# Feed-forward gate and up as 2x2 block products: seven products of 256 columns for eight

## The chip, the cores and the metric

The kernel runs on one core of one Trainium2 chip. It is a two-layer model step in one launch. Time is device time in microseconds (us) of that core; lower is better. TensorE does the matrix products (the profile lists matmuls as PE, weight loads as PEld), VectorE is DVE, ScalarE is ACT, GpSimd is POOL, and SyncE (SP) issues most transfers. Each engine works through its own queue in order and waits on semaphores for the others.

## The reference

```python
# x: 512 tokens, D_MODEL = 1024, D_FF = 2816, all float32
def swiglu(x, w_gate, w_up, w_down):
    return (jax.nn.silu(x @ w_gate) * (x @ w_up)) @ w_down
...
x = x + concat([o_nsa, o_mla], axis=-1) @ ev_w_out[i]          # layer 0: attention mixers
x = x + swiglu(rms_norm(x, ev_ffn_norm[i]), ffn_w_gate[i], ffn_w_up[i], ffn_w_down[i])
...
x = x + short_conv_mixer(u, b_g, c_g, conv_w[i]) @ od_w_out[i]  # layer 1
x = x + moe_swiglu(rms_norm(x, od_ffn_norm[i]), ...)
```

The change is in the `swiglu` of layer 0 alone.

## The kernel before

The stages follow each other: attention mixers, their output projection (`out_rest`), the feed-forward part, the convolution layer, the experts. Every fp32 matrix product is made of three: each operand is split into a rounded part `hi` and a remainder `lo`, and `mm3` issues hi·hi, hi·lo and lo·hi into one PSUM sum. A split is one ACT cast (`hi`) and one DVE subtraction (`lo`).

**Weights.** `Weights` holds one list of pieces for the whole kernel in the order of use. A piece arrives by an SP transfer of 512 KB (128x1024) in one of six raw buffers (`wbr0` to `wbr5`), is split into one of six part buffers (`wap0` to `wap2`, `wbp0` to `wbp2`), and then its raw buffer takes the next transfer. `done(...)` gives part buffers back and calls `pump`, which writes down the next transfers and splits in each engine's queue at that place of the program. So the order of `done` calls sets where a split stands between other work.

**Feed-forward part.** `FFN_ORDER` lists 22 "up" tiles (128 of the 2816 columns of gate and of up, all 512 tokens) and six "down" products: up 0, 1, 2, 3, down of tiles 0 and 1, then runs of four up tiles with a down of four tiles behind each, and at last up 20, 21 and a down of 18 to 21. Tiles 0 and 1 go through `first`, in products of 256 tokens, with the transposes of the last two token blocks between them. Tiles 2 to 21 take `product_of_next` for gate and again for up (8 blocks of depth 128, three matmuls of 512 columns each, so 48 matmuls a tile), and `ff_tile`:

```python
ACT.activation(sg, pg, AF.Silu)
DVE.tensor_tensor(sg, pu, sg, op=OP.mult)
split(hT[f][:, 0], hT[f][:, 1], sg)
```

**Ahead of it.** `out_rest` interleaves the output projection with the norm of each of four token blocks: squares on ACT, a sum on DVE, a power on POOL (`rs`, in `norm.factor`), the scaling to `xn` on DVE (`norm.scale`), PE transposes of `xn` into PSUM (`pt`), and the split of those into the activations `b0h`, `b0l`, `b1h`, `b1l`. Transposes 0 and 1 are in `out_rest`, 2 and 3 in `first`. POOL has nothing but the four powers there.

Of the kernel before, what the change touches and what calls it, by code (L numbers as in the profile page):

```python
# [302 lines left out]
class Weights:  # L303
# [22 lines left out]
    def add_part(self, src, offset, row, at, k, n, keep=False):  # L326

        self.pieces.append(Piece(len(self.chunks), 0, k, n, keep))
        self.chunks.append((bass.AP(tensor=src.tensor, offset=src.offset + offset + at, ap=[[row, 128], [1, k * n]]), k * n))

    def pump(self, pieces=99):

        while True:
            if self.loaded < len(self.chunks) and self.raw_free:
                ap, m = self.chunks[self.loaded]
                pool, tag = slot = self.raw_free.pop(0)
                t = pool.tile([128, PW], F32, name=tag, tag=tag, bufs=1)
# [3 lines left out]
            elif (pieces and self.ready < len(self.pieces) and self.pieces[self.ready].chunk in self.raw  # L341
                  and self.part_free):
                pieces -= 1
                p = self.pieces[self.ready]
                self.ready += 1
                raw, raw_slot = self.raw[p.chunk]
                pool, tag = p.slot = self.part_free.pop(0)
                p.t = pool.tile([128, 2, PW], F32R, name=tag, tag=tag, bufs=1)
                m = p.k * p.n
                src = raw[:, p.at:p.at + m]  # L350
                self.nc.scalar.copy(p.t[:, 0, :m], src)  # L351
                self.nc.vector.tensor_tensor(p.t[:, 1, :m], src, p.t[:, 0, :m].bitcast(F32), op=OP.subtract)  # L352
                if p.keep:
                    p.raw, p.raw_slot = self.raw.pop(p.chunk)
                else:
                    self.raw_free.append(self.raw.pop(p.chunk)[1])
            else:
                return

    def use(self):  # L360

        while self.ready <= self.used:
            before = self.ready
            self.pump(1)
            assert self.ready > before
        self.used += 1
        return self.pieces[self.used - 1]

    def done(self, *pieces, splits=99):
        self.part_free += [p.slot for p in pieces]  # L370
        self.pump(splits)

    def let_go(self, *pieces):
# [12 lines left out]
class Piece:  # L386
# [40 lines left out]
def kernel(ctx: ExitStack, tc: tile.TileContext, A, out, stop=None):  # L427
# [32 lines left out]
    def weight_room(name, raw, parts):  # L460
        W.room(wx.enter_context(tc.tile_pool(name=name, bufs=1, side="right")), raw, parts)
# [23 lines left out]
    og = od = 0  # L485
    for do, f in FFN_ORDER:
        if do == "up":
            og = W.add(A["w_gu"], og, (KD, 128), (KD, 128))
# [91 lines left out]
    with ExitStack() as l0:  # L580
# [686 lines left out]
        oT = Act.of([b() for b in oh], [b() for b in ol])  # L1267
        W.resume(len(chunk_bufs), 3)

    weight_room("wb", 6, 3)  # L1270
    rt = wx.enter_context(tc.tile_pool(name="rt", bufs=1, side="right"))
    psA = ctx.enter_context(tc.tile_pool(name="psA", bufs=4, space=PSUM))
# [136 lines left out]
        return p  # L1409

    def ff_tile(f, pg, pu):
        sg = work.tile([128, T], F32, name="sg", bufs=2)
        hT[f] = work.tile([128, 2, T], F32R, name="hT", tag="hT", bufs=6)
        ACT.activation(sg, pg, AF.Silu)
        DVE.tensor_tensor(sg, pu, sg, op=OP.mult)
        split(hT[f][:, 0], hT[f][:, 1], sg)

    def ff_down(f0, nf, mid, end):
# [47 lines left out]

    def conv_tile(j, pc, pu, pb):
        z = zs[j % 2]
        ct = work.tile([128, T], F32, name="sg", bufs=2)
# [63 lines left out]
    def transpose(i):  # L1533

        hl = split_rows[i] = [work.tile([128, KD, 128], F32R, name="hT", tag="hT", bufs=6) for _ in range(2)]
        for b in range(2):
            pt = psA.tile([128, 4, 128], F32, name="pt", tag="p")
            for j in range(4):
                k = 4 * b + j
                PE.transpose(pt[:, j], xr[i][:, k * 128:(k + 1) * 128], ident)  # L1540
            split(hl[0][:, 4 * b:4 * b + 4], hl[1][:, 4 * b:4 * b + 4], pt)

    def logits(i):
        h, l = split_rows.pop(i)
# [7 lines left out]
        lT = work.tile([16, 128], F32, name="sg", bufs=2)  # L1552
        ACT.copy(lT, p)
        return lT

# [477 lines left out]
```

## Time and profile before

| | |
|---|---|
| median of 3 runs | 1367.07 us (1365.72 to 1367.53) |
| the profiled execution's own time | 1367.42 us |
| its span | 1365.7 us |
| PE busy in the span | 1332.3 us (98%) |
| DVE, ACT, POOL busy | 844.6 us (62%), 688.8 us (50%), 208.2 us (15%) |
| stretch 358 to 691 us (up tiles 2 to 21 and downs): PE, DVE, ACT, POOL busy | 333.00, 131.53, 88.11, 1.65 of 333 us |
| granted TensorE clock, whole span | 0.994 of full speed |

The span is the part of the execution in which instructions ran; the 1.7 us beside it lie outside. A matmul's recorded duration overlaps the next one's, so the pace of PE is read from the distance of starts, not from the durations. A row of the timeline gives start, duration, engine, line, operation, output<-inputs with the shape, and in brackets how long the engine had been idle and for whom it waited.

### The profile page before, as it was taken

How to read it: one execution, taken by the hardware profiler on the slowest of the kernel's cores; microseconds unless marked ns; L12 is line 12 of the kernel's file. 1: busy time of each engine (PE TensorE's matmuls, PEld its weight loads, DVE VectorE, ACT ScalarE, POOL GpSimd, SP SyncE). 2: the span in 40 equal slices, each digit the busy share in tenths (PEclk: the TensorE clock that was granted, in tenths of full speed). 3: DMA queues.
4: the chain of work that ended last, by engine and by line, in shares of the span. 5: the costliest groups of instructions: out<-in, count | busy, mean ns of one | idle time of the engine just before them, and what ended most of it. 6: DMA issues, size and time to landing. Idle time of an engine off the chain costs nothing. (4 is left out here: it accounts for less than half of the span.)

```text
span 1365.7 us, 19159 instructions
## 1 busy us (share of the span) xinstructions
PE 1332.3 (98%) x6956; PEld 1061.4 (78%) x6957; DVE 844.6 (62%) x1365; ACT 688.8 (50%) x1144; POOL 208.2 (15%) x309
## 2 busy tenths in 40 slices
PE   7999899999999999999999999999999999999997
PEld 6866687879888888888898888888877878677774
DVE  4348897956433433434355444588888789786864
ACT  4535887854322222222242222377767678575763
POOL 2257554320000000000000000020111101201001
PEclk9999999999999999999999999999999999999999
DMA  5243101123321313132233222299997989979692
GB/s 191 88 157 113 32 17 47 47 101 124 116 93 63 131 61 133 62 124 75 95 109 108 93 93 78 103 340 321 401 341 258 358 326 399 324 250 338 231 342 53
DMA packets 69175, 229.83 MB, mean 168 GB/s; under 512 B 8768, under 2 KB 10060, under 8 KB 69068
## 3 DMA queue, kind: packets, MB, share of 16 engines
q1 hardware_dynamic: 64332, 217.39, 44.4%
q0 software_dynamic: 3392, 9.48, 2.9%
q10 hardware_dynamic: 1344, 1.58, 0.4%
q8 instruction: 62, 1.02, 0.3%
q14 instruction: 45, 0.37, 0.1%
HBM read 219.47 MB, written 8.94 MB: 167 GB/s over the span
## 5 line engine op out<-in xcount | busy, mean ns | idle before, releaser
L352 DVE TENSOR_TENSOR wbp<-wbr,wbp 128x1024 fp32r<-128x1024 f32 (+2 forms) x91 | 107.3, 1194 | 145.1 <-ACT wbp L351 143.2
L351 ACT CAST wbp<-wbr 128x1024 fp32r<-128x1024 f32 (+2 forms) x91 | 92.1, 1026 | 203.5 <-PE pg L515 109.1
L352 DVE TENSOR_TENSOR wap<-wbr,wap 128x1024 fp32r<-128x1024 f32 (+1 forms) x88 | 103.6, 1192 | 96.2 <-ACT wap L351 95.1
L351 ACT CAST wap<-wbr 128x1024 fp32r<-128x1024 f32 (+1 forms) x88 | 89.5, 1027 | 113.0 <-PE pg L515 73.5
L352 DVE TENSOR_TENSOR wap<-wcr,wap 128x1024 fp32r<-128x1024 f32 (+2 forms) x84 | 90.9, 1114 | 16.5 <-ACT wap L351 10.9
L352 DVE TENSOR_TENSOR wbp<-wcr,wbp 128x1024 fp32r<-128x1024 f32 (+2 forms) x83 | 91.6, 1129 | 12.4 <-ACT wbp L351 10.6
L524 POOL TENSOR_TENSOR rs<-rs,mhalf 128x1 f32<-128x1 f32 x11 | 6.1, 551 | 566.4 <-DVE rs L523 566.4
L351 ACT CAST wap<-wcr 128x1024 fp32r<-128x1024 f32 (+2 forms) x84 | 78.4, 962 | 18.7 <-DMA wcr<-w_eg 9.2
L351 ACT CAST wbp<-wcr 128x1024 fp32r<-128x1024 f32 (+2 forms) x83 | 79.4, 977 | 16.0 <-DMA wcr<-w_eg 6.5
L513 PE MATMUL pg<-wap,xgTh 128*128 128x512 f32 (+1 forms) x168 | 64.1, 382 | 0.7
L513 PE MATMUL pg<-wbp,xgTh 128*128 128x512 f32 (+1 forms) x162 | 61.7, 381 | 1.0
L515 PE MATMUL pg<-wap,xgTl 128*128 128x512 f32 (+1 forms) x168 | 62.5, 372 | 0.0
L514 PE MATMUL pg<-wap,xgTh 128*128 128x512 f32 (+1 forms) x168 | 62.4, 372 | 0.0
L514 PE MATMUL pg<-wbp,xgTh 128*128 128x512 f32 (+1 forms) x162 | 60.3, 372 | 0.0
L515 PE MATMUL pg<-wbp,xgTl 128*128 128x512 f32 (+1 forms) x162 | 60.3, 372 | 0.0
L1434 DVE TENSOR_TENSOR x<-pd,x 128x512 f32<-128x512 f32 x48 | 32.3, 689 | 39.2 <-PE pd L515 39.1
L612 POOL TENSOR_TENSOR s<-s,mhalf 128x4 f32<-128x4 f32 (+4 forms) x37 | 35.3, 963 | 70.2 <-DVE s L611 55.6
L1735 POOL DMA_INDIRECT xg<-xd,idx x15 | 22.9, 1530 | 140.6 <-DVE idx L1694 120.0
L636 DVE TENSOR_TENSOR wap<-r,wap 128x1024 fp32r<-128x1024 f32 (+3 forms) x24 | 26.2, 1091 | 26.5 <-ACT wap L633 26.4
L1897 POOL DMA_INDIRECT out_dram<-y,idx x7 | 14.9, 2128 | 174.5 <-ACT xe L1760 174.5
L513 PE MATMUL pd<-wap,hT 128*128 128x512 f32 x104 | 41.2, 396 | 0.0
L515 PE MATMUL pd<-wap,hT 128*128 128x512 f32 x104 | 41.1, 395 | 0.0
(531 smaller groups left out, 3926.4 us busy)
## 6 DMA issues: line engine op xcount, KB each, us to landing
wcr<-w_ed SPq DMA_DIRECT2D x50, 512.0 KB
wcr<-w_eg SPq DMA_DIRECT2D x45, 512.0 KB
wbr<-w_gu SPq DMA_DIRECT2D x44, 512.0 KB
wcr<-w_eu SPq DMA_DIRECT2D x40, 512.0 KB
wbr<-w_ed SPq DMA_DIRECT2D x30, 512.0 KB
wbr<-w_od_in SPq DMA_DIRECT2D x24, 512.0 KB
wbr<-w_eu SPq DMA_DIRECT2D x24, 512.0 KB
wbr<-w_down SPq DMA_DIRECT2D x22, 512.0 KB
```

The costliest lines, as they stand in the source:

```text
L351: self.nc.scalar.copy(p.t[:, 0, :m], src)
L352: self.nc.vector.tensor_tensor(p.t[:, 1, :m], src, p.t[:, 0, :m].bitcast(F32), op=OP.subtract)
L513: PE.matmul(o, lh, rh, start=start, stop=False)
L514: PE.matmul(o, lh, rl, start=False, stop=False)
L515: PE.matmul(o, ll, rh, start=False, stop=stop)
L524: POOL.tensor_tensor(dst, dst, mhalf[:p, :m], op=OP.pow)
L612: op("POOL", 70 + 78 * n, lambda: POOL.tensor_tensor(rs(), rs(), mhalf[:rs().shape[0], :n], op=OP.pow), (), [buf])
L636: op("DVE", m, lambda: DVE.tensor_tensor(p.t[:, 1, :m], src(), p.t[:, 0, :m].bitcast(F32), op=OP.subtract), [raw], [part])
L1434: DVE.tensor_tensor(x[i][:, cs], ps[c], x[i][:, cs], op=OP.add)
L1735: POOL.indirect_dma_start(out=t, out_offset=None, in_=src, in_offset=rows_of(e, b, n))
L1897: POOL.indirect_dma_start(out=out, out_offset=rows_of(e, 0), in_=y, in_offset=None, compute_op=OP.add)
```

## The change

Tiles 2 to 21 (`PLAIN = 2`) are computed by `ff_products` with the Strassen scheme in Winograd's form. The left matrix is [gate | up] (rows) by the two halves of the depth (columns), the right one the two depth halves by the two token halves. Seven products of 4 depth blocks, three matmuls of 256 columns each (84 matmuls a tile), replace eight such products in four sums.

- Weight sums: three POOL subtractions or additions of 128x512 when a tile's two raw chunks are in (`sums`), and a fourth after the second split (`split`, j == 1). The seven left operands are split into halves of part buffers, so a tile takes four part buffers.
- Activation sums, made once: `unsplit` on POOL gives back hi + lo (four of 128x1024), `right_sums` on DVE makes four differences of 128x1024, and each is split.
- The sums of the products: one ACT copy, and DVE additions of two 128x512 and three 128x256 out of PSUM; then Silu, product and split of 128x512 as before.
- In tile 2 the sixth product, which needs no activation sum, is moved ahead of the third.

```diff
+    def add_products(self, src, offset, scratch):
+        for m in range(2):
+            self.chunks.append((bass.AP(tensor=src.tensor, offset=src.offset + offset + m * PW,
+                                        ap=[[2 * PW, 128], [1, PW]]), PW))
+        g = self.groups[len(self.chunks) - 1] = Products(self.nc, len(self.chunks) - 2, scratch)
+        self.pieces += g.pieces
+        return offset + 128 * 2 * PW
...
                 self.nc.sync.dma_start(t[:, :m], ap)
                 self.raw[self.loaded] = t, slot
+                if self.loaded in self.groups:
+                    self.loaded_groups.append(self.groups[self.loaded])
+                    self.sum_up()
...
+                if isinstance(p, Operand):
+                    slot = None if p.j % 2 else self.part_free.pop(0)
+                    for chunk in p.group.split(p, slot):
+                        self.raw_free.append(self.raw.pop(chunk)[1])
+                    if p.j == 3:
+                        self.summed -= 1
+                        self.sum_up()
+                    continue
...
+    def sum_up(self):
+        while self.loaded_groups and self.summed < 2:
+            self.summed += 1
+            g = self.loaded_groups.pop(0)
+            g.sums(*(self.raw[g.chunk + m][0] for m in range(2)))
...
+class Products:
...
+    def sums(self, a, b):
+        h = PW // 2
+        s3, s2 = self.scratch()
+        add = self.nc.gpsimd.tensor_tensor
+        add(s3, a[:, :h], b[:, :h], op=OP.subtract)
+        add(b[:, :h], b[:, :h], b[:, h:], op=OP.add)
+        add(s2, b[:, :h], a[:, :h], op=OP.subtract)
+        self.s2 = s2
+        self.src = [a[:, :h], a[:, h:], s2, s3, b[:, :h], a[:, h:], b[:, h:]]
+    def split(self, p, slot):
...
+        nc.scalar.copy(p.t[:, 0], self.src[j])
+        nc.vector.tensor_tensor(p.t[:, 1], self.src[j], p.t[:, 0].bitcast(F32), op=OP.subtract)
+        if j == 1:
+            nc.gpsimd.tensor_tensor(self.src[5], self.src[1], self.s2, op=OP.subtract)
+        return {5: [self.chunk], 6: [self.chunk + 1]}.get(j, [])
...
+    def unsplit(s):
+        for kb in range(2):
+            w = whole[kb, s] = work.tile([128, 4, T // 2], F32, name="whole", tag="hT", bufs=6)
+            POOL.tensor_tensor(w, xT.h[kb][:, :, tok2[s]].bitcast(F32), xT.l[kb][:, :, tok2[s]].bitcast(F32), op=OP.add)
+    def right_sums():
+        t1, t3, t4, t2 = whole[0, 0], whole[0, 1], whole[1, 0], whole[1, 1]
+        for dst, a, b in ((t1, t3, t1), (t3, t2, t3), (t2, t2, t1), (t4, t4, t2)):
+            DVE.tensor_tensor(dst, a, b, op=OP.subtract)
+        for j, t in ((2, t2), (3, t3), (1, t1), (4, t4)):
+            split(sums[j - 1][:, 0], sums[j - 1][:, 1], t)
+    RIGHT = [Half(0, 0), Half(1, 0), Sum(2), Sum(3), Sum(1), Half(1, 1), Sum(4)]
+    def ff_products(f):
+        two = [128, 2, T // 2]
+        c, a, b, d = (psB.tile(two, F32, name="pg", tag="g") for _ in range(4))
+        place = [c[:, 0], a[:, 0], a[:, 1], b[:, 0], b[:, 1], d[:, 0], d[:, 1]]
+        r = work.tile([128, 5, T // 2], F32, name="R", bufs=2)
...
+        go(0)
+        ACT.copy(r[:, 4], c[:, 0])
+        go(1)
+        W.done(ws[0], ws[1])
+        late = f == PLAIN
+        if late:
+            go(5)
+        go(2)
+        add(r[:, 0:4:2], a, r[:, 4:5].to_broadcast(two))
+        go(3)
+        W.done(ws[2], ws[3])
+        go(4)
+        add(r[:, 3:5], b, r[:, 2:3].to_broadcast(two))
+        if not late:
+            go(5)
+        add(r[:, 1], d[:, 0], r[:, 4])
+        ACT.activation(r[:, 0:2], r[:, 0:2], AF.Silu)
+        add(r[:, 4], b[:, 1], r[:, 3])
+        W.done(ws[4], ws[5])
+        go(6)
+        add(r[:, 3], d[:, 1], r[:, 3])
+        h = r[:, 0:2]
+        DVE.tensor_tensor(h, r[:, 3:5], h, op=OP.mult)
...
     nothing = lambda i: None
-    late = {0: lambda: transpose(2), 1: lambda: transpose(3)}
+    unsplit(0)
+    late = {0: lambda: transpose(2), 1: lambda: transpose(3), 2: lambda: unsplit(1)}
...
-        elif f > 1:
-            pg = product_of_next()
-            ff_tile(f, pg, product_of_next())
+        elif f >= PLAIN:
+            if f == PLAIN:
+                right_sums()
+            ff_products(f)
```

Three places of the engines' queues show where the new work stands. First POOL's queue at the output projection, before (`a1l` is the end of the attention part, `rs_3509` to `rs_3621` are the powers of the four token blocks here, `rs_5859` is the first one at the end of the feed-forward part):

```order
L1113 TENSOR_TENSOR a1l_3093<-v0_3392,a1h_3055 128x512
L524 TENSOR_TENSOR rs_3509<-rs_3509,mhalf_77 128x1
L524 TENSOR_TENSOR rs_3532<-rs_3532,mhalf_77 128x1
L524 TENSOR_TENSOR rs_3586<-rs_3586,mhalf_77 128x1
L524 TENSOR_TENSOR rs_3621<-rs_3621,mhalf_77 128x1
L524 TENSOR_TENSOR rs_5859<-rs_5859,mhalf_77 128x1
```

and with the change (`sum` and the `wbr` outputs are the weight sums of tiles 2 and 3, `rs` the same four powers):

```order
L1199 TENSOR_TENSOR a1l_3093<-v0_3392,a1h_3055 128x512
L461 TENSOR_TENSOR sum_3489<-wbr5_3482,wbr0_3487 128x512
L462 TENSOR_TENSOR wbr0_3487<-wbr0_3487 128x512
L463 TENSOR_TENSOR sum_3490<-wbr0_3487,wbr5_3482 128x512
L610 TENSOR_TENSOR rs_3514<-rs_3514,mhalf_77 128x1
L610 TENSOR_TENSOR rs_3537<-rs_3537,mhalf_77 128x1
L461 TENSOR_TENSOR sum_3577<-wbr1_3521,wbr2_3575 128x512
L462 TENSOR_TENSOR wbr2_3575<-wbr2_3575 128x512
L463 TENSOR_TENSOR sum_3578<-wbr2_3575,wbr1_3521 128x512
L610 TENSOR_TENSOR rs_3596<-rs_3596,mhalf_77 128x1
L610 TENSOR_TENSOR rs_3631<-rs_3631,mhalf_77 128x1
```

The three sums of tile 2 stand ahead of the powers of token blocks 0 and 1, and those of tile 3 ahead of the powers of blocks 2 and 3. The four `unsplit` follow after them.

Second, DVE's queue where tile 1 ends and tile 2 begins, before (`sg` and `hT` are `ff_tile`, the `wap` and `wbp` rows are weight splits for later pieces):

```order
L352 TENSOR_TENSOR wap_3862<-wbr_3628,wap_3862 128x1024
L352 TENSOR_TENSOR wap_3891<-wbr_3633,wap_3891 128x1024
L1415 TENSOR_TENSOR sg<-pg,sg 128x512
L519 TENSOR_TENSOR hT<-sg,hT 128x512
L352 TENSOR_TENSOR wap_3927<-wbr_3791,wap_3927 128x1024
L352 TENSOR_TENSOR wbp_3957<-wbr_3796,wbp_3957 128x1024
```

and with the change (`whole` are the four differences, `t_` their splits, `R<-pg` the sums of tile 2's products):

```order
L1502 TENSOR_TENSOR sg<-pg,sg 128x512
L605 TENSOR_TENSOR hT<-sg,hT 128x512
L1553 TENSOR_TENSOR whole<-whole 128x1024 x4
L605 TENSOR_TENSOR t_3647<-whole,t_3647 128x1024
L605 TENSOR_TENSOR t_3648<-whole,t_3648 128x1024
L605 TENSOR_TENSOR t_3646<-whole,t_3646 128x1024
L605 TENSOR_TENSOR t_3649<-whole,t_3649 128x1024
L477 TENSOR_TENSOR wap_3975<-wbr_3575,wap_3975 128x512
L477 TENSOR_TENSOR wap_3975<-wbr_3521,wap_3975 128x512
L1575 TENSOR_TENSOR R<-pg,R 128x2x256
```

Eight instructions of 128x1024 now stand between tile 1's last split and everything that follows.

Third, DVE's queue for up tiles in the middle of a run, before (tiles 6 and 7):

```order
L352 TENSOR_TENSOR wap0_4295<-wbr4_4131,wap0_4295 128x1024
L1415 TENSOR_TENSOR sg_4300<-pg_4270,sg_4300 128x512
L519 TENSOR_TENSOR hT_4301<-sg_4300,hT_4301 128x512
L352 TENSOR_TENSOR wap1_4331<-wbr5_4136,wap1_4331 128x1024
L352 TENSOR_TENSOR wbp0_4361<-wbr0_4166,wbp0_4361 128x1024
L1415 TENSOR_TENSOR sg_4366<-pg_4336,sg_4366 128x512
L519 TENSOR_TENSOR hT_4367<-sg_4366,hT_4367 128x512
```

and with the change (tile 9; the `wap`, `wbp` rows are operands of tiles 10 and 11):

```order
L477 TENSOR_TENSOR wbp2_5042<-sum_4779,wbp2_5042 128x512
L477 TENSOR_TENSOR wap2_5077<-wbr4_4721,wap2_5077 128x512
L477 TENSOR_TENSOR wap2_5077<-wbr3_4691,wap2_5077 128x512
L1575 TENSOR_TENSOR R_5051<-pg_5048,R_5051 128x2x256
L477 TENSOR_TENSOR wap0_5109<-wbr4_4721,wap0_5109 128x512
L1575 TENSOR_TENSOR R_5051<-pg_5049,R_5051 128x512
L1575 TENSOR_TENSOR R_5051<-pg_5050,R_5051 128x256
L1575 TENSOR_TENSOR R_5051<-pg_5049,R_5051 128x256
L477 TENSOR_TENSOR wap1_5142<-wbr5_4881,wap1_5142 128x512 x2
L1575 TENSOR_TENSOR R_5051<-pg_5050,R_5051 128x256
L1600 TENSOR_TENSOR R_5051<-R_5051 128x512
L605 TENSOR_TENSOR hT_5161<-R_5051,hT_5161 128x512
```

Two splits of 128x1024, one product and one split of 128x512 a tile have become seven splits of 128x512, five additions out of PSUM, one product and one split.

## Rows read from the trace of the kernel before

**Rows 1.** Busy time by stretch: engines, granted clock, DMA share, GB/s.
```profile
358.00:691.00 333.00, 333.00 (x1446) 270.02 (x1445) 131.53 (x152) 88.11 (x108) 1.65 (x3) 1.00 0.27 90
```

**Rows 2.** Timeline of PE: first matmul of three runs of four up tiles.
```profile
378.66 0.40 PE L513 MATMUL pg<-b0h,wap 128*128 128x512 f32 x1
...
445.86 0.40 PE L513 MATMUL pg<-b0h,wap 128*128 128x512 f32 x1
...
512.22 0.40 PE L513 MATMUL pg<-b0h,wap 128*128 128x512 f32 x1
```

**Rows 3.** Timeline of PE in `first`: two matmuls of 256 columns, 120 apart.
```profile
331.00 0.28 PE L513 MATMUL pg<-b1h,wap 128*128 128x256 f32 x1
...
345.13 0.28 PE L513 MATMUL pg<-b1h,wap 128*128 128x256 f32 x1
```

**Rows 4.** Timeline of DVE: two splits in a row, one behind a cast, one of 1024.
```profile
319.87 0.68 DVE L519 TENSOR_TENSOR b0l<-pt,b0h 128x512 fp32r<-128x512 f32 x1
320.47 0.68 DVE L519 TENSOR_TENSOR b1l<-pt,b1h 128x512 fp32r<-128x512 f32 x1
...
344.45 0.69 DVE L519 TENSOR_TENSOR hT<-sg,hT 128x512 fp32r<-128x512 f32 x1 [0.69 <-ACT hT L518]
345.40 1.22 DVE L352 TENSOR_TENSOR wap<-wbr,wap 128x1024 fp32r<-128x1024 f32 x1 [0.26 <-ACT wap L351]
```

**Rows 5.** Line 1113 on POOL: subtractions of two sizes, ns min/median/max.
```profile
L1113 POOL TENSOR_TENSOR a0l<-u,a0h x8: 732/736/742, 166.8 to 236.4; 128x256 fp32r<-128x256 f32 x8
L1113 POOL TENSOR_TENSOR a1l<-v,a1h x4: 1282/1286/1289, 269.3 to 294.4; 128x512 fp32r<-128x512 f32 x4
```

**Rows 6.** Timelines of POOL and DVE where both read two SBUF operands.
```profile
133.93 0.32 POOL L938 TENSOR_TENSOR qm<-rt 128x64 f32<-128x64 f32 x1
...
135.01 1.34 POOL L938 TENSOR_TENSOR qm<-rt 128x64 f32<-128x64 f32 x1
...
134.95 1.23 DVE L636 TENSOR_TENSOR wap<-r,wap 128x1024 fp32r<-128x1024 f32 x1
...
260.10 2.22 POOL L1207 TENSOR_SCALAR T<-T,s 128x512 f32<-128x512 f32 x2 [3.16 <-DVE s L1206]
...
260.44 1.43 DVE L636 TENSOR_TENSOR wap<-r,wap 128x1024 fp32r<-128x1024 f32 x1
...
110.91 4.46 POOL L612 TENSOR_TENSOR s<-s,mhalf 128x4 f32<-128x4 f32 x5 [0.18 <-DVE s L611]
...
112.94 0.43 DVE L1000 TENSOR_TENSOR km<-km,s 128x256 f32<-128x256 f32 x1 [0.21 <-POOL s L612]
```

**Rows 7.** Timelines of POOL and SP, and a stretch of DMA, at the norms.
```profile
308.97 0.56 POOL L524 TENSOR_TENSOR rs<-rs,mhalf 128x1 f32<-128x1 f32 x1 [13.25 <-DVE rs L523]
...
320.10 0.55 POOL L524 TENSOR_TENSOR rs<-rs,mhalf 128x1 f32<-128x1 f32 x1 [6.59 <-DVE rs L523]
...
305.24 0.33 SPq L338 DMA_DIRECT2D wbr<-w_gu  x1
...
319.32 0.33 SPq L338 DMA_DIRECT2D wbr<-w_gu  x1
...
308.00:310.00 2.00, 2.00 (x10) 1.63 (x9) 1.19 (x3) 1.75 (x5) 0.56 (x1) 1.00 0.05 21
```

**Rows 8.** Timelines of PE and DVE: transposes 0 and 2, and the scaling before transpose 2.
```profile
310.91 1.09 PE L570 MATMUL pt<-ident,xn 128*128 128x128 f32 x8
...
323.95 1.04 PE L570 MATMUL pt<-ident,xn 128*128 128x128 f32 x8
...
321.93 1.28 DVE L557 SCALAR_TENSOR_TENSOR xn<-x,rs,gain 128x1024 f32<-128x1024 f32 x1
```

**Rows 9.** Timeline of PE after its longest idle time: matmuls 1 and 13.
```profile
294.57 0.47 PE L513 MATMUL po<-wap,a1h 128*128 128x512 f32 x1 [3.08 <-DVE x L1261]
...
298.99 0.40 PE L513 MATMUL po<-wap,a1h 128*128 128x512 f32 x1
```

**Rows 10.** Timeline of DVE: the last split of tile 1.
```profile
349.32 0.69 DVE L519 TENSOR_TENSOR hT<-sg,hT 128x512 fp32r<-128x512 f32 x1 [0.69 <-ACT hT L518]
```

More of the change, by code (lines that the diff above doesn't have):

```diff
@@ L369, in done @@
     def done(self, *pieces, splits=99):
-        self.part_free += [p.slot for p in pieces]
+        self.part_free += [p.slot for p in pieces if p.slot]
         self.pump(splits)
@@ L397, in whole, with __init__, hi, lo @@
         return self.raw[:, k * self.n:(k + 1) * self.n]
+class Operand:
+    def __init__(self, group, j, chunk):
+        self.group, self.j, self.chunk, self.slot = group, j, chunk, None
+    def hi(self, k):
+        return self.t[:, 0, k * 128:(k + 1) * 128]
+    def lo(self, k):
+        return self.t[:, 1, k * 128:(k + 1) * 128]
+class Products:
+    def __init__(self, nc, chunk, scratch):
+        self.nc, self.chunk, self.scratch = nc, chunk, scratch
+        self.pieces = [Operand(self, j, chunk + 1) for j in range(7)]
+        self.src = None
+    def sums(self, a, b):
[8 more added lines that the diff above has]
+    def split(self, p, slot):
+        h, j, nc = PW // 2, p.j, self.nc
+        if slot:
+            pool, tag = self.slot = slot
+            self.t = pool.tile([128, 2, PW], F32R, name=tag, tag=tag, bufs=1)
+        if j % 2 or j == 6:
+            p.slot = self.slot
+        p.t = self.t[:, :, h * (j % 2):h * (j % 2) + h]
+        nc.scalar.copy(p.t[:, 0], self.src[j])
[3 more added lines that the diff above has]
+        return {5: [self.chunk], 6: [self.chunk + 1]}.get(j, [])
 class Act:
@@ L487 @@
         if do == "up":
-            og = W.add(A["w_gu"], og, (KD, 128), (KD, 128))
+            if f < PLAIN:
+                og = W.add(A["w_gu"], og, (KD, 128), (KD, 128))
+            else:
+                og = W.add_products(A["w_gu"], og, lambda f=f: scratch(f))
         else:
@@ L1268 @@
         W.resume(len(chunk_bufs), 3)
+    scratch = lambda f: [work.tile([128, PW // 2], F32, name="sum", tag=t, bufs=n) for t, n in (("y", 2), (f"z{f % 2}", 1))]
     weight_room("wb", 6, 3)
@@ L1411, in ff_tile @@
     def ff_tile(f, pg, pu):
-        sg = work.tile([128, T], F32, name="sg", bufs=2)
+        sg = work.tile([128, T], F32, name="sg", tag="R", bufs=2)
         hT[f] = work.tile([128, 2, T], F32R, name="hT", tag="hT", bufs=6)
@@ L1438, in ff_down, with __init__ @@
             del hT[f0 + f]
+    sums = [act.tile([128, 2, 4, T // 2], F32R, name=f"t{j + 1}", tag=t, bufs=1)
+            for j, t in enumerate(("a0h", "a0l", "a1h", "a1l"))]
+    tok2 = [slice(0, T // 2), slice(T // 2, T)]
+    class Half:
+        def __init__(self, kb, s):
+            self.hi = lambda k: xT.hi(4 * kb + k, tok2[s])
+            self.lo = lambda k: xT.lo(4 * kb + k, tok2[s])
+    class Sum:
+        def __init__(self, j):
+            self.hi = lambda k: sums[j - 1][:, 0, k]
+            self.lo = lambda k: sums[j - 1][:, 1, k]
@@ new lines @@
+    whole = {}
+    def unsplit(s):
[8 more added lines that the diff above has]
+            split(sums[j - 1][:, 0], sums[j - 1][:, 1], t)
@@ new lines, with go, add @@
+    RIGHT = [Half(0, 0), Half(1, 0), Sum(2), Sum(3), Sum(1), Half(1, 1), Sum(4)]
[4 more added lines that the diff above has]
+        r = work.tile([128, 5, T // 2], F32, name="R", bufs=2)
+        ws = []
+        def go(j):
+            while len(ws) <= j:
+                ws.append(W.use())
+            for k in range(4):
+                mm3(place[j], ws[j].hi(k), ws[j].lo(k), RIGHT[j].hi(k), RIGHT[j].lo(k), k == 0, k == 3)
+        def add(dst, x, y):
+            DVE.tensor_tensor(dst, x, y, op=OP.add)
+        go(0)
[19 more added lines that the diff above has]
+        add(r[:, 3], d[:, 1], r[:, 3])
+        hT[f] = work.tile([128, 2, T], F32R, name="hT", tag="hT", bufs=6)
+        h = r[:, 0:2]
+        DVE.tensor_tensor(h, r[:, 3:5], h, op=OP.mult)
+        two_of = lambda j: hT[f][:, j].rearrange("p (a t) -> p a t", a=2)
+        split(two_of(0), two_of(1), h)
+        W.done(ws[6])
@@ L1468, in conv_tile @@
         z = zs[j % 2]
-        ct = work.tile([128, T], F32, name="sg", bufs=2)
+        ct = work.tile([128, T], F32, name="ct", tag="R", bufs=2)
         ACT.copy(ct, pc)
@@ L1551, in logits @@
                 PE.matmul(p, wr[:, k], h[:, k], start=False, stop=k == KD - 1)
-        lT = work.tile([16, 128], F32, name="sg", bufs=2)
+        lT = work.tile([16, 128], F32, name="lT", tag="R", bufs=2)
         ACT.copy(lT, p)
```

8 lines of the change are left out of this document (7 added, 1 removed).

## The prediction

> **What bounds the kernel now.** Read the busy times by stretch first: over the up tiles and downs PE is busy 333.00 of 333 us at the full granted clock (1.00, the level of 2.4 GHz), DVE for 131.5, ACT for 88.1, POOL for 1.65 [rows 1]. No engine is waited for there. So each matmul less is worth its pace, and new work on DVE, ACT and POOL costs nothing until PE has to wait for it. Next come starts of PE, not durations. Two runs of four up tiles and a down lie between 378.66 and 512.22, so one takes 66.78 us for 4 x 48 + 96 = 288 matmuls of 512 columns: 0.2319 us each, 11.13 us an up tile [rows 2]. The new matmuls have 256 columns; `first` has the same ones, with the same splits and half banks: 120 in 14.13 us, 0.1177 us each [rows 3].
>
> **What PE gains.** 84 x 0.1177 = 9.89 us a tile for 11.13: 1.24 us less, 24.9 us over 20 tiles. It is less than an eighth because 256 columns cost slightly more than half of 512 (0.1177 against 0.1160).
>
> **First cost: POOL's queue at the norms.** The queue is served in order, and the sums of tile 2 stand ahead of the powers of blocks 0 and 1. They need the second chunk of tile 2, whose transfer is issued at 305.24; in the stretch from 308 the DMA engines are nearly idle (0.05), so it has landed by about 308.1, 2.8 us after issue [rows 7]. A POOL subtraction of 128x512 takes 1.286 us, one of 256 0.736 [rows 5]. Those write fp32r and the new ones plain fp32, but a plain product of 64 columns, 0.32 [rows 6], lies on the same line of 0.19 + 2.15 ns a column. So I take 1.286, and as the lower end 1.10, if the fixed part of one overlaps the one before. Three take 3.9 us, to 312.0, where the power began at 308.97 [rows 7]: 3.1 us late (2.5 at the lower end). The chain behind it has no slack: the transposes start at 310.91, and the scaling ended there [rows 8]. PE waits 3.1 us.
>
> The sums of tile 3 stand ahead of the powers of blocks 2 and 3, and wait for a transfer issued at 319.32 before [rows 7], now at 322.4, since all is 3.1 later. It lands 2.8 later at 325.2; three sums end at 329.1; the power (0.55) and the scaling (1.28) end at 331.0. Transpose 2, at 323.95 before [rows 8], would be due at 327.05. PE waits 3.9 us (3.3 at the lower end). The last power follows directly, and 2.8 us of products lie ahead of transpose 3.
>
> **Second cost: the activation sums.** `unsplit` is off the path: transpose 3 follows transpose 2 by a product of 2.8 us, so it ends some 16 us ahead of tile 2 [rows 3, 8], and of the four POOL additions of 1024 (an estimate: 2.4 us each, twice 1.286 less one fixed part) only two come behind it. `right_sums` is not: it stands in DVE's queue behind the last split of tile 1, which starts at 349.32 [rows 10], 4.2 us after the last matmul of `first` (tile 2 began at 345.13 [rows 3]). In front of product 3 PE has products 1, 2 and 6, 36 matmuls, 4.2 us. DVE needs the rest of that split (0.6), four differences (1.13 each in a row: 1.22 less the overlap of 0.09 [rows 4]) and one split of 1.22, whose cast runs beside the fourth difference: 6.4 us. 4.2 + 6.4 - 4.2, some 0.6 less because the splits just ahead are shorter: PE waits 5.8 us. The other three splits come at 1.13 us each, ahead of products of 1.41. Bounds: 5.0 if the weight splits ahead save 1.4 rather than 0.6, 8.5 if the weight sums of tile 4, due about then, block two or three of these.
>
> **Third cost: the clock.** After its longest idle time, 3.08 us, PE needs 4.42 us for twelve matmuls that should take 2.78: 1.6 us lost at the level of 1.2 GHz [rows 9]. I take that twice, for the two longer waits: 3.2 us; bounds 0 and 4.8.
>
> **Fourth cost: the up tiles themselves.** DVE's seven splits, two sums, product and last split of 512 are 0.60 apart in a row [rows 4], 11 x 0.60 = 6.6; the three sums of 256 are 0.34 each (0.60 less half of the 0.53 between a split of 1024 and one of 512). That is 7.6 us. DVE also sits idle twice a tile for ACT, as for the cast now (0.69 [rows 4]): once for Silu and a cast behind it, once for the cast of the result, with small gaps about 2.0. So 9.6 us of DVE against 9.89 of PE: DVE just follows, where it was at 40%. ACT has about 5 us of work a tile and is no bound.
>
> On top comes POOL. DVE and POOL hold each other up where both read two SBUF operands: a POOL product of 0.32 took 1.34 and ended 0.17 after a DVE subtraction that began just before it, and a DVE split, 1.22 alone, took 1.43 when a POOL instruction was running [rows 6]. The powers of POOL, 0.9 us each, do not hold DVE: one of its products took 0.43 in the middle of them [rows 6]. So what counts is the time in which data stream: for 512 columns 1.10 us (from the two sizes of [rows 5]). The Trainium skill (SBUF — State Buffer, Who interferes with whom) has it stricter: the one that issues second is blocked for the whole instruction of the other. By that rule each sum costs DVE up to 1.29 us; the powers here do not bear it out, the streams do.
>
> A run of four tiles has 16 sums; some 11 fall between its start and its last drains, the others into the down. DVE is in a stretch that does not read two SBUF operands (sums out of PSUM 2.2, idle 1.5) for 3.7 of 9.6 us, so I take 0.6 of 1.10, 0.66 us, for the delay d of each. Against PE, DVE falls behind by 11 d, plus 2.4 for the four splits that only start after a down, less 4 x 0.29: 1.2 + 11 d = 8.5 us by the fourth tile. What is late first are the sums out of PSUM: a bank's last reader comes after product 6 and the bank is written again by product 4 of the next tile, four products or 5.6 us on; in the fourth tile nothing waits for banks before the down, and its third weight row is due 2.8 us into it. I take 7.8 us as what may be late unseen. So 0.7 us a run, 3 us over four runs. The last down needs tile 21 itself, 4.2 us after it begins: 1 us.
>
> **Sum**, against the profiled execution's 1367.4 us: -24.9 + 3.1 + 3.9 + 5.8 + 3.2 + 3 + 1 = -4.9, so 1362.5. The median of the runs is 0.35 under the profiled one: **1362 us**.
>
> **Rivals.**
> - DVE is overrun by POOL's sums. If d is the whole 1.10, a run is 13.3 us behind, 5.5 over what is hidden: 22 us in four runs instead of 3, 1381 us. For it speaks that DVE has only 0.3 us of air a tile, against it that the sums in the downs and in DVE's gaps are free. It decides from d = 0.87 on: then the runs lose 12 us and the total is over 1369.8. By the rule of the Trainium skill cited above d is at most 1.29: 30 us, 1389.
> - The waits at the norms do not come: the two chunks land early enough that POOL is through with the sums when a power is due. Then only the 5.8 us of `right_sums` and no clock loss remain: 1367.4 - 24.9 + 5.8 = 1348 us. Against it: the chunk of tile 2 cannot land before its raw buffer is free, at 305.24, and the transposes follow the scaling at once [rows 7, 8].
> - The change does not do what it says: 256 columns are paced by something else than in `first` (by the weight loads, say, now that the left operand changes with each product of 12 instead of 24). At 0.1325 us a matmul all gain is gone, and with the other costs the total is 1387. Against it: in `first` too each matmul loads its weights, at 0.1177 [rows 3].
>
> **Chances.** Forecast 0.55, with its own range 1355 to 1369; overrun 0.25; no waits at the norms 0.15; slow matmuls 0.05. No change that can be told apart lies within 0.2%, 2.7 us, of 1367.1. The forecast's case falls below 1364.3 about 0.38, within 0.14, above 0.03; no waits at the norms all below; the overrun within 0.05 and above 0.20; slow matmuls above. Together faster 0.53, same 0.19, slower 0.28. The range leaves out some 0.1 on each side: 1349 to 1380.
>
> **What would show it.** In the new profile: 12 matmuls of a product 1.41 us from start to start; transposes 0 and 2 with an idle time of PE of 2 to 4 us each, the power ahead of them right behind the sums; PE idle 5 to 8.5 us ahead of the third product of tile 2, released by a split of `t2`; granted clock under 1 after these. In the runs of four: PE hardly idle, DVE's sums out of PSUM later by the tile and on time again after a down. The prediction is wrong if PE waits in each run for DVE (then d was too small), or if the powers are not behind the sums in time.

## The result: slower by 3.5%, and the profile after

The changed kernel takes 1414.7 us (median of 4 runs, 1414.1 to 1415.9) against 1367.3 (4 runs); ratio 1.035, 95% interval 1.033 to 1.037. 1362 was forecast, and the top of the range was 1380. The span is 1412.4 us instead of 1365.7. PE is busy for 94% of it instead of 98%, DVE for 70% instead of 62%.

Five stretches, each from one first matmul to the next, show where it went:

| stretch | before, us | after, us | difference | forecast |
|---|---|---|---|---|
| norms and tiles 0, 1: [rows 9] to the first matmul of tile 2 [rows 3] | 50.56 | 63.52 | +13.0 | +10.2 |
| tiles 2, 3 and the down of 0, 1, to the first run of four [rows 2] | 33.53 | 49.26 | +15.7 | +3.3 |
| four runs of four tiles and a down | 267.12 | 284.21 | +17.1 | -16.8 |
| tiles 20, 21 | 22.40 | 22.28 | -0.1 | -2.5 |
| last down, with the next norms | 24.18 | 24.23 | +0.1 | +1.0 |

The clock's 3.2 us stand in the first row of the forecast. If the prediction's "two longer waits" are those of 3.9 and 5.8 us, half of it belongs to the second row (8.6 and 4.9); the sum is the same.

The waits of PE come first (engine and line, what it waited for: us in total, times, longest), from the projection to the end of the feed-forward part. Before, PE waited there 3.1 us once for `x` and 0.3 for a split; both are still there.

```profile
PE pg L599 <- DVE R L1575: 33.7, 20, 3.5
PE pg L599 <- ACT t L604: 7.8, 1, 7.8
PE pt L656 <- DVE rs L609: 4.2, 1, 4.2
PE pt L656 <- DVE xn L643: 4.1, 1, 4.1
...
PE pg L600 <- DVE t L605: 0.7, 1, 0.7
```

The first row is the one that was not forecast: 20 waits for a sum out of PSUM (`R`, line 1575), one in each of the 20 tiles. The timeline of PE shows them (these rows answer to [rows 2, 3, 8]):

```profile
314.83 1.52 PE L656 MATMUL pt<-ident,xn 128*128 128x128 f32 x8 [4.13 <-DVE xn L643]
...
333.75 1.94 PE L656 MATMUL pt<-ident,xn 128*128 128x128 f32 x8 [4.15 <-DVE rs L609]
...
357.90 0.28 PE L599 MATMUL pg<-b0h,wap 128*128 128x256 f32 x1
...
359.32 0.28 PE L599 MATMUL pg<-b1h,wap 128*128 128x256 f32 x1
...
370.10 0.58 PE L599 MATMUL pg<-t,wbp 128*128 128x256 f32 x1 [7.80 <-ACT t L604]
...
416.41 0.36 PE L599 MATMUL pg<-t,wbp 128*128 128x256 f32 x1 [0.61 <-DVE R L1575]
...
427.15 0.35 PE L599 MATMUL pg<-t,wap 128*128 128x256 f32 x1 [0.61 <-DVE R L1575]
...
476.38 0.28 PE L599 MATMUL pg<-b0h,wap 128*128 128x256 f32 x1
...
522.55 0.36 PE L599 MATMUL pg<-t,wbp 128*128 128x256 f32 x1 [3.28 <-DVE R L1575]
...
524.42 0.63 PE L599 MATMUL pd<-wap,hT 128*128 128x512 f32 x1
...
548.06 0.28 PE L599 MATMUL pg<-b0h,wbp 128*128 128x256 f32 x1
```

Twelve matmuls take 1.42 us (357.90 to 359.32), as forecast. But the seventh product of every tile waits: 0.61 us at the least, so that a tile takes 10.74 us (416.41 to 427.15) instead of 9.89. In the last tile of each run of four, and in the first tile of three of the four runs, it waits 2.75 to 3.5 us. The run from 476.38 to 548.06 has 2.75 + 0.61 + 0.87 + 3.28 = 7.5 us of such waits, and its down takes 23.64 instead of 22.40 us. The reason for the 1.24 stands in the windows (columns as in [rows 1]): the granted clock is 0.63 in the 4 us behind the wait of 3.28.

```profile
476.38:548.06 71.68, 64.17 (x434) 58.77 (x433) 52.07 (x69) 25.05 (x44) 24.05 (x16) 0.98 0.27 90
...
522.50:526.50 4.00, 3.95 (x17) 3.55 (x18) 3.21 (x5) 1.60 (x3) 3.29 (x3) 0.63 0.40 130
```

Why a product waits for a sum is in the code: `place` puts products 6 and 7 into the two halves of one PSUM tile, `d`, and DVE's `add(r[:, 1], d[:, 0], r[:, 4])` reads the first half while product 7 is due to write the second. The program has PE wait for that read, though the columns are others. The Trainium skill (PSUM — Partial Sum Buffer, PSUM bank collisions raise a hardware error) asks for it: PSUM is to be guarded by bank, not by address. The trace shows what this guard costs here, 0.61 us of idle time in a tile at the least; what would happen without it, no run here shows. So in this program a bank that is still read holds PE from the next product on, not from the next tile on.

What makes the read late stands on DVE and POOL just ahead of 522.55:

```profile
514.98 4.56 DVE L374 TENSOR_TENSOR wap<-wbr,wap 128x1024 fp32r<-128x1024 f32 x2
...
521.20 1.67 DVE L1575 TENSOR_TENSOR R<-pg,R 128x512 f32<-128x512 f32 x3
```
```profile
514.59 1.63 POOL L462 TENSOR_TENSOR wbr<-wbr 128x512 f32<-128x512 f32 x1
516.30 2.16 POOL L463 TENSOR_TENSOR sum<-wbr,wbr 128x512 f32<-128x512 f32 x1
```

Two splits that take 2.36 us alone took 4.56 beside POOL's sums; the three sums out of PSUM follow in one piece of 1.67 us, the one out of `d` second, ended about 522.2 (0.60 for the one of 512, 0.4 for that of 256), and PE went on at 522.55.

### The profile page after: what moved, and what is told of

Same layout as the page of the kernel before. It is cut to its first block, busy times and chain, and to the rows that moved or that the text cites. A ratio compares the mean times of both kernels' runs of the same rounds, so it can differ in the third digit from the quotient of the medians.

```text
span 1412.4 us, 21218 instructions
## 1 busy us (share of the span) xinstructions
PE 1327.3 (94%) x7676; PEld 1091.3 (77%) x7677; DVE 995.5 (70%) x1573; ACT 733.8 (52%) x1268; POOL 341.8 (24%) x393
## 3 DMA queue, kind: packets, MB, share of 16 engines
q8 instruction: 68, 1.11, 0.3%
## 5 line engine op out<-in xcount | busy, mean ns | idle before, releaser
L374 DVE TENSOR_TENSOR wbp<-wbr,wbp 128x1024 fp32r<-128x1024 f32 (+1 forms) x72 | 90.1, 1259 | 50.2 <-ACT wbp L373 50.2
L374 DVE TENSOR_TENSOR wap<-wbr,wap 128x1024 fp32r<-128x1024 f32 (+2 forms) x67 | 84.4, 1280 | 46.8 <-ACT wap L373 45.0
L373 ACT CAST wbp<-wbr 128x1024 fp32r<-128x1024 f32 (+1 forms) x72 | 72.8, 1019 | 56.5 <-PE pg L601 16.9
L373 ACT CAST wap<-wbr 128x1024 fp32r<-128x1024 f32 (+2 forms) x67 | 67.2, 1018 | 49.1 <-PE pg L601 21.8
L599 PE MATMUL pg<-t,wbp 128*128 128x256 f32 x184 | 54.4, 296 | 32.8 <-DVE R L1575 25.0
L599 PE MATMUL pg<-wbp,xgTh 128*128 128x512 f32 (+1 forms) x166 | 63.5, 382 | 0.7
L599 PEld LDWEIGHTS pg<-t,wbp 128*128 128x128 f32 x184 | 36.3, 197 | 35.7 <-issue 27.7
L477 DVE TENSOR_TENSOR wap<-wbr,wap 128x512 fp32r<-128x512 f32 x61 | 52.6, 899 | 15.3 <-ACT wap L476 15.2
L479 POOL TENSOR_TENSOR wbr<-wbr,sum 128x512 f32<-128x512 f32 x20 | 28.1, 1405 | 142.8 <-DVE wap L477 75.2
L600 PE MATMUL pg<-wbp,xgTh 128*128 128x512 f32 (+1 forms) x166 | 61.9, 373 | 0.8 <-DVE wbp L374 0.8
L461 POOL TENSOR_TENSOR sum<-wbr,wbr 128x512 f32<-128x512 f32 x20 | 30.4, 1518 | 113.9 <-DMA wbr<-w_gu 87.4
```

What stands on the lines that cost most here:

```text
L461: add(s3, a[:, :h], b[:, :h], op=OP.subtract)
L477: nc.vector.tensor_tensor(p.t[:, 1], self.src[j], p.t[:, 0].bitcast(F32), op=OP.subtract)
L479: nc.gpsimd.tensor_tensor(self.src[5], self.src[1], self.s2, op=OP.subtract)
L599: PE.matmul(o, lh, rh, start=start, stop=False)
L600: PE.matmul(o, lh, rl, start=False, stop=False)
```

## The experiments

Theory T: the bank that products 6 and 7 share turns DVE's lag into waits. Rival R: DVE, held by POOL, is itself the bound, and PE will wait for it at one place or another.

**1. The seventh product in a bank of its own.**

```diff
+        e = psA.tile(two, F32, name="p7", tag="p")
-        place = [c[:, 0], a[:, 0], a[:, 1], b[:, 0], b[:, 1], d[:, 0], d[:, 1]]
+        place = [c[:, 0], a[:, 0], a[:, 1], b[:, 0], b[:, 1], d[:, 0], e[:, 0]]
```

> Only the PSUM bank of the seventh product is changed: it gets a bank of its own instead of the second half of the sixth product's bank. Theory T (the shared bank makes PE wait at once for any lag of DVE: 33.7 us of waits at the seventh product, and a clock below 1 behind each of the longer ones, 1.25 us in each down): these waits go, a run of four tiles and a down falls from 71.7 us to 62 to 63, as the pace of 0.1177 us a matmul asks, and the total falls by 40 to 48 us, to 1367 to 1375. Rival R (DVE with GpSimd beside it is itself the bound): PE waits elsewhere for the same lag, a run stays at 69 us or more, and the total falls by less than 12 us, 1403 or more.

1395.9 us (ratio to before 1.021, 1.019 to 1.022): 19 us back, between the two theories. The waits in the tiles are gone but for one of 0.7 us, and a tile takes 9.9 us, but each down in the middle now waits (waits from 385 us on, then PE and DVE in one run):

```profile
PE pd L599 <- DVE R L1576: 14.2, 5, 3.7
...
PE pg L599 <- DVE R L1576: 0.7, 1, 0.7
```
```profile
511.09 0.39 PE L599 MATMUL pd<-wap,hT 128*128 128x512 f32 x1
...
521.48 0.50 PE L599 MATMUL pd<-wap,hT 128*128 128x512 f32 x1 [2.94 <-DVE R L1576]
```
```profile
521.45 1.54 DVE L1601 TENSOR_TENSOR R<-R 128x512 f32<-128x512 f32 x1
```

The seventh product of the last tile ends as the down begins, at 511.09; DVE's product of that tile starts 10.4 us later. The down's fourth sum takes the bank of that seventh product and waits for its reader. T found the place of the wait, R that the lag is real.

**2 and 3. No weight sums on POOL, with the shared bank and with the bank of its own.** In tiles 4 to 21 (`plain`) the raw halves are the operands, so these compute something else; the experts behind them then take another time (1784 us in all, and 1770 in the one run of the second), and only the feed-forward stage is read.

```diff
+        if self.plain:
+            self.src = [a[:, :h], a[:, h:], a[:, :h], b[:, :h], b[:, :h], a[:, h:], b[:, h:]]
+            return
```

> Leaves out GpSimd's weight sums of tiles 4 to 21 (the operands are the raw halves, so those tiles compute something else); the bank of products 6 and 7 stays shared. Theory T: the seventh product still waits in each tile, for the time DVE needs to read the sixth (0.61 us at the least, 12 us over 20 tiles), but hardly more, since GpSimd no longer holds DVE; the clock in the downs stays at 1. A run of four falls from 71.7 us to 65 to 67, the total to 1385 to 1395. Rival R (GpSimd holding DVE is the cause, the bank is not): no wait is left at the seventh product, a run is 62 to 63 us, the total 1372 to 1380.

> Leaves out GpSimd's weight sums of tiles 4 to 21 (those tiles compute something else, and what follows on their values takes another time, so only the feed-forward stage is read), with the seventh product in a bank of its own. It shows what DVE does without GpSimd beside it. Theory B: no wait of PE is left in the runs, a run and its down takes 61.9 to 62.3 us (4 x 9.89 + 22.4), DVE is busy for 43.3 of them. Rival R (DVE alone cannot follow at 256 columns): PE waits 2 us or more in each run.

A run and its down, first with the shared bank, then with its own (windows of two kernels):

```profile
464.68:530.36 65.68, 63.01 (x433) 57.91 (x432) 43.30 (x69) 25.14 (x44) 0.00 (x0) 1.00 0.29 97
```
```profile
501.03:563.09 62.06, 62.06 (x434) 57.66 (x433) 42.66 (x69) 25.08 (x44) 0.00 (x0) 1.00 0.30 102
```

So the two causes can be set side by side, in us for a run of four and its down (66.8 before the change; 4 x 9.89 + 22.40 = 61.96 by the pace alone). With POOL's sums the second to fourth runs are given; the first takes 69.2 and 64.0:

| | shared bank | own bank |
|---|---|---|
| with POOL's sums | 71.6 to 71.7 | 66.1 to 67.3 |
| without | 65.6 to 65.7 | 62.06 |

The bank alone costs 3.6 us a run, the sums alone 4 to 5, both together 9.6, more than the two added. Without the sums DVE follows PE, as forecast, and the shared bank still makes PE wait 0.61 us in each tile and 0.84 to 1.11 in the last of a run, as T had it. DVE is busy for 52.07 us of a run with the 16 sums and 43.30 without: a sum costs DVE 0.55 us.

**4. The powers of the norms ahead of the sums of tiles 2 and 3.**

```diff
-        while self.loaded_groups and self.summed < 2:
+        while not self.hold and self.loaded_groups and self.summed < 2:
...
+    W.hold = False
+    W.sum_up()
     unsplit(0)
```

> GpSimd's weight sums of tiles 2 and 3 are written behind the four powers of the norms instead of ahead of them; nothing else is changed. Theory T (GpSimd's queue delays transposes 0 and 2 by 4.13 and 4.15 us, and the clock behind them costs the rest of the 12.2 us by which transpose 3 is late): transpose 3 is back within 1 us of its time before the change, and the total falls by 10 to 13 us, to 1402 to 1405, if the sums, now later, do not hold up DVE's activation sums. Rival: the sums run into the splits and activation sums of tile 2, the wait of 7.8 us ahead of its third product grows by 3 us or more, and the total falls by less than 9.

1408.8 us (1.031, 1.029 to 1.032): 5.9 us back. Both waits at the norms are gone (transpose 3 at 326.55, where it was at 327.65 before the change and 340.00 with it). The rival is right that the work behind is held up and that less than 9 us come back, but not in the place: the wait ahead of tile 2's third product did not grow (7.3 us). A new wait of 5.0 us stands ahead of its first product. POOL's six sums and four `unsplit` come one after the other from 322.98 to 345.29, the fourth sum of tile 2 only then; ACT waits for it with a cast until 346.54, and the Silu of tile 1, which frees the bank for PE, stands behind that cast.

```profile
349.64 0.58 PE L600 MATMUL pg<-b0h,wap 128*128 128x256 f32 x1 [5.01 <-ACT sg L1502]
...
364.08 0.58 PE L600 MATMUL pg<-t,wbp 128*128 128x256 f32 x1 [7.26 <-ACT t L605]
```

**5. Tiles 2 and 3 plain, with the bank of its own.** PE then has plain products to do while DVE makes the activation sums; the sixth product is moved ahead of the third in no tile.

```diff
-PLAIN = 2
+PLAIN = 4
...
+            if f == 2:
+                right_sums()
             pg = product_of_next()
```

> The seventh product has a bank of its own, and tiles 2 and 3 are computed plainly (18 tiles in products instead of 20); the activation sums are written ahead of tile 2's plain products, so that PE has 22 us of work while DVE makes them. Theory T: beside the waits at the seventh product, the waits at transposes 0 and 2 and the one ahead of the third product go (the weight sums of tile 4 stand behind the powers), with their clock loss. Two tiles at the old pace cost 2.5 us. Against the run with the bank alone the total falls by 12.2 + 7.8 + 0.7 + about 1 - 2.5 = 18 to 20 us: 1348 to 1356, faster than before the change. Rival: the first product tile follows the down directly and its operands are not split in time, or the activation sums delay the splits of tiles 2 and 3; then PE waits there and the gain over the bank alone is under 12 us.

1369.6 us (1.0016, 1.0006 to 1.0025): 26 us less than experiment 1, where 18 to 20 were expected, but not faster than before the change. Its ten runs lie between 1367.0 and 1375.6 us, and the trace is of the slowest. In it, from [rows 9] to the first run of four it takes 89.1 us, experiment 1 113.3, the kernel before 84.1. It still waits 10.6 us in four downs and 2.5 in the first.

**6, 7 and 8. Another bank for the last seventh product; and `unsplit` later.** In the last tile of a run the seventh product takes the free half `c[:, 1]` of the first product's bank: once in the kernel of experiment 1, once in that of 5, and there once more with all four `unsplit` ahead of tile 2's plain products and `right_sums` behind them.

```diff
-        e = psA.tile(two, F32, name="p7", tag="p")
+        e = c[:, 1] if f % 4 == 3 or f == NF - 1 else psA.tile(two, F32, name="p7", tag="p")[:, 0]
```

> As the run with the seventh product in a bank of its own, but in the last tile of each run of up tiles the seventh product takes the free half of the first product's bank, so that the down's sums never ask for a bank that DVE has still to read. Theory B (the waits that were left, 2.9 us in each down, are again for a bank: the down's fourth sum takes the bank of the last seventh product): they go, a run and its down takes 62 to 63 us instead of 66, and the total falls from 1395.9 to 1374 to 1381. Rival R (DVE is behind with all it does, and PE waits for it at the next place, operands or hidden values): the waits of PE between 390 and 700 us stay above 8 us, and the total stays above 1389.

> The same change of banks in the kernel with two more plain tiles and the activation sums ahead of them. Theory B: the four waits of 2.9 us in the downs go with their clock loss (a run of 68.4 us becomes 62 to 63), and the total falls from 1369.6 to 1350 to 1357, faster than before the change by about 1%. Rival R: waits for DVE of 8 us or more stay in the downs, and the total stays above 1364.

> As the previous one, and GpSimd's four additions that give back hi + lo, which hold DVE's scaling and splits in the first tiles (1.28 us became 3.41, two splits 2.36 became 4.52, and PE waited 1.9 us for a split and 2.5 us in the first down), are written into tile 2's plain products, the activation sums behind them. Theory: both waits go, with some clock loss, and the total falls by another 3 to 6 us, to 1345 to 1353. Rival: the activation sums, now later in DVE's queue, delay the splits of tiles 3 and 4, PE waits in the down of tiles 0 and 1 or at tile 4, and the total does not fall.

1395.5, 1369.9 and 1375.2 us: the rivals held, twice with no gain, once with a loss (the trace of the third is of its slowest run, 1379.9 us). The wait moved on to the next bank: the down's fifth sum takes that of the first, which DVE adds to `x` behind all it has still to do for the last tile (waits of experiments 6 and 8; the 9.9 us are in the down of tiles 0 and 1).

```profile
PE pd L599 <- DVE x L1521: 16.7, 5, 5.7
```
```profile
PE pd L599 <- DVE x L1521: 19.4, 5, 9.9
```

So DVE has to be less late, not the banks further off. In experiment 5 DVE's product starts 4.2, 4.9 and 6.0 us behind the first three seventh products of a run and about 10 behind the fourth (2.1, 2.1, 2.4 and 3.1 without POOL's sums, in experiment 3): in the fourth tile the splits of the down's weights meet seven sums.

**9. The last tile of each run plain** (tiles 7, 11, 15, 19), in the kernel of experiment 5: 14 tiles in products.

```diff
-            if f < PLAIN:
+            if f < PLAIN or f % 4 == 3:
```

> As the run with two more plain tiles and the seventh product in a bank of its own, but the last tile of each run of four (7, 11, 15, 19) is computed plainly too, so 14 tiles in products are left. DVE is furthest behind in that tile (9.6 to 10.3 us from the end of the seventh product to DVE's product, against 4.2 to 6.0 in the three tiles ahead of it), since the splits of the down's weights and seven of GpSimd's sums fall together there. Theory D (what is left of the loss is DVE's lag in the last tile of a run): four tiles at the old pace cost 5.0 us, the waits in four downs (9.8 us) and some 4 us of clock go: 1357 to 1366, faster than before. Rival (the lag only moves to the next place, as it did twice): PE waits 2 us or more in each run and the total stays above 1367.

1357.0 us: 0.992 of before (0.991 to 0.994), and no wait of PE is left in the four runs.

**10. The weight sums in the downs.** The kernel of experiment 7, with POOL's sums for the next run held back until the down has added its first token block to `x`; POOL waits by an instruction that reads that block, and `release` is called by the down behind each block.

```diff
+    def release(i):
+        if i == 0:
+            POOL.tensor_tensor(gate, x[0][:, :1], mhalf[:, :1], op=OP.mult)
+            W.hold = False
+            W.sum_up()
+        elif i == 1:
+            W.pump()
...
+            if f % 4 == 2:
+                W.hold = True
             ff_products(f)
```

> As the run with two more plain tiles and the last seventh product in the first product's bank, but GpSimd's weight sums for the next run wait until the down has added its first token block to x, so they run in the down, where DVE has little to do, and so do the splits that need them. Theory D: without these sums beside it DVE is 5 to 6 us behind in the last tile instead of 10, the waits of 2.8 us in the downs go, and so does their clock loss: 1352 to 1361 us, faster than before by 0.5% or more. Rival: sums and splits come too late for the first tile of the next run, PE waits there for operands, 2 us or more in each run, and the total stays above 1366.

1353.8 us: 0.990 of before (0.988 to 0.992). PE's windows and the end of one run, with DVE's product:

```profile
484.94:547.12 62.18, 62.18 (x434) 57.53 (x433) 52.75 (x69) 24.87 (x45) 23.91 (x17) 1.00 0.31 103
```
```profile
484.94 0.39 PE L600 MATMUL pd<-wap,hT 128*128 128x512 f32 x1
```
```profile
489.52 0.69 DVE L1602 TENSOR_TENSOR R<-R 128x512 f32<-128x512 f32 x1
```

The same two places in experiment 7:

```profile
486.70 0.40 PE L599 MATMUL pd<-wap,hT 128*128 128x512 f32 x1
```
```profile
496.32 1.57 DVE L1601 TENSOR_TENSOR R<-R 128x512 f32<-128x512 f32 x1
```

DVE is as busy as with the change (52.75 us of a run), but 4.6 us late at the end of the run instead of 9.6 to 10.0 in experiment 7 (7.8 in its first run), and PE never waits in the runs. Only the place of the sums, and of the splits that need them, differs from experiment 7, so their bunching in the last tile is shown as the cause of what was left.

**11. The first two `unsplit` behind the last two**, in the kernel of experiment 10.

```diff
-    unsplit(0)
-    late = {0: lambda: transpose(2), 1: lambda: transpose(3), 2: lambda: unsplit(1)}
+    late = {0: lambda: transpose(2), 1: lambda: transpose(3), 2: lambda: (unsplit(1), unsplit(0))}
```

> As the run with GpSimd's sums in the downs, but the two additions that give back hi + lo of the first token half stand behind those of the second half, which wait for the last transposes, so no GpSimd addition runs beside DVE's last scaling and the two splits behind it (3.41 and 4.52 us there instead of 1.28 and 2.36). Theory (GpSimd holds DVE while both read two SBUF operands, for nearly the whole of its instruction): the scaling takes 1.28 us again, PE's wait of 1.9 us for the split goes with the clock behind it, and the total falls by 2 to 4 us, to 1350 to 1352. Rival: the same additions hold the next splits, a wait of 1.5 us or more appears within the first tiles or the first down, and the total stays within 1 us of 1353.8.

1352.5 us (0.989, 0.988 to 0.991), the lowest median of all, between what theory and rival expected. DVE's last scaling and the two splits behind it, before and with this edit (experiment 10, then 11):

```profile
323.71 3.41 DVE L644 SCALAR_TENSOR_TENSOR xn<-x,rs,gain 128x1024 f32<-128x1024 f32 x1 [0.73 <-POOL rs L611]
327.04 4.52 DVE L375 TENSOR_TENSOR wap<-wbr,wap 128x1024 fp32r<-128x1024 f32 x2
```
```profile
324.18 1.29 DVE L644 SCALAR_TENSOR_TENSOR xn<-x,rs,gain 128x1024 f32<-128x1024 f32 x1 [0.73 <-POOL rs L611]
325.38 2.36 DVE L375 TENSOR_TENSOR wap<-wbr,wap 128x1024 fp32r<-128x1024 f32 x2
```
```profile
375.42 0.50 PE L600 MATMUL pd<-wap,hT 128*128 128x512 f32 x1 [2.18 <-DVE x L1522]
```

The wait of 1.9 us is gone, as expected, but the one in the first down grew from 0.8 to 2.2, as the rival had it; 1.3 us remain. The intervals of experiments 10 and 11 overlap, so that gain in the total is not shown; the shorter scaling and splits are.

## Why the prediction was wrong, step by step

- **Pace of 256 columns: right.** 1.42 us for twelve matmuls, 62.06 us for a run where nothing waits (61.96 by that pace). The rival on the pace falls.
- **What may be late unseen (7.8 us a run): this step failed.** It took a bank's last reader to have four products of air, 5.6 us, and overlooked that products 6 and 7 share a bank, where there is none. So DVE's lag was not hidden but paid in each tile: 33.7 us of waits, and five of the eight long ones (2.75 us and more) took clock with them. Experiments 1 to 3 show it. The step was too kind a second time: it had the down wait for weights alone, but with the bank apart (experiments 1 and 6) the down's own sums wait for banks that DVE has still to read, 2.8 to 2.9 us in three of five downs. By experiment 1 some 5.4 us could be late unseen there, not 7.8 (an estimate: the product starts 10.4 us behind, 2.1 of which is no lag, and PE waits 2.9).
- **The delay by POOL's sums (d = 0.66): nearly right**, 0.55 us. At the end of a run the sums add 7.3 us of lag (10.4 in experiment 1 against 3.1 in experiment 3), where 11 d = 7.3 were forecast; the whole lag, from the 2.1 us of a tile on time to 10.4, is 8.3 for 8.5. So PE waits in each run, the prediction's own sign of being wrong, but not because d was too small, as it says there: the lag came as forecast, and the banks did not bear it. The rival "overrun", with d = 1.10 and deciding from 0.87, has the right sign for the wrong reason. The delay was also taken as even over the run: in fact seven sums meet in the last tile, which experiment 10 undid.
- **Waits at the norms: right, too small.** 4.13 and 4.15 us for 3.1 and 3.9. The first sum began at 308.95 instead of 308.1 and the power followed the three sums at once:

```profile
308.95 1.30 POOL L461 TENSOR_TENSOR sum<-wbr,wbr 128x512 f32<-128x512 f32 x1 [13.42 <-DVE rs L609]
...
312.89 0.56 POOL L610 TENSOR_TENSOR rs<-rs,mhalf 128x1 f32<-128x1 f32 x1
...
331.73 0.55 POOL L610 TENSOR_TENSOR rs<-rs,mhalf 128x1 f32<-128x1 f32 x1
```

  Experiment 4 adds that they were not worth their sum: what DVE and POOL do behind them was nearly as late without them.
- **`right_sums`: right, too small.** 7.80 + 0.73 us for 5.8, at the bound of 8.5: the four differences took 6.06 us, where 4.6 were reckoned, and tile 1's last split ahead of them 1.75 instead of 0.69, both beside POOL's sums. The reason named for that bound, the weight sums of tile 4, is the right one: experiment 2 leaves them out, the differences take 5.00 us there, the split 0.69, and the first wait is 5.83:

```profile
366.27 0.58 PE L603 MATMUL pg<-t,wbp 128*128 128x256 f32 x1 [5.83 <-ACT t L608]
```

- **Clock: too small.** 3.2 us were forecast, for two waits; the granted clock was 0.57, 0.50 and 0.50 in the 4 to 5 us behind the waits at 314.83, 333.75 and 370.10, where PE lost about 1.7, 2.6 and 2.5 us by the starts of its matmuls, and each of the five downs in the middle lost 1.2 to 1.3 us.
- **The last down (1 us)**: not seen in the changed kernel, where tile 21 is already held up by its own bank; 1.0 to 1.7 us where the bank is apart.

## What to carry to other kernels

Ahead of any figure for slack, list for each PSUM bank who reads it last and which matmul writes into any part of it next: in this program two halves of a bank are one buffer, and a reader of one half holds the writer of the other. Where an engine goes from 38% of a run to 73% busy, look at its load tile by tile rather than in the mean; what was late at the end of a run came from work that could stand elsewhere. And when a wait is removed and comes back at the next bank, it is the late engine that needs relief, not the bank.

## What the runs showed of the hardware that was not expected

- DVE loses nearly all that is left of a POOL instruction where both read two SBUF operands. In experiment 1 the product at 521.45 began 0.29 us into a POOL sum of 1.28 and took 1.54 us instead of 0.69, so it lost 0.85 of the 0.99 us that were left. Twelve products of the changed kernel met a sum so, and each ended 0.54 to 0.56 us behind the sum's end. The scaling at 323.71 in experiment 10 took 3.41 us instead of 1.29: 2.12 of the 2.33 us left of an addition of 1024 columns. POOL's sums grew too, from 1.29 to 1.6 and 2.16.

```profile
521.16 1.28 POOL L479 TENSOR_TENSOR wbr<-wbr,sum 128x512 f32<-128x512 f32 x1 [0.63 <-DVE wbp L477]
```
```profile
323.64 2.40 POOL L1548 TENSOR_TENSOR whole<-b0h,b0l 128x1024 f32<-128x1024 f32 x1
```

  The Trainium skill (SBUF — State Buffer, Who interferes with whom) has the later one blocked for the whole instruction of the earlier; these rows come near it (0.85 of 0.99, 2.12 of 2.33). The powers of [rows 6] still stand against it for POOL instructions in general.
- A wait of nearly the same length cost clock or did not. With the change the granted clock stayed at 1.00 behind the waits in the first tile of a run (2.75, 3.02 and 2.76 us at 487.77, 559.39 and 631.07) and was 0.63 to 0.65 in the 4 us behind those in the last (2.85 to 3.51 us); in experiment 1 it was 1.00 behind one wait of 2.94 us (521.48) and 0.63 behind another (587.18). What decides it was not tried.
